# Summing the up-projection's weight blocks in device memory for the second MLP too, and running it with two plain groups instead of three

## The chip, the cores and the metric

The kernel runs on one core of one Trainium2 chip. All inputs and the output lie in device memory. The metric is the device time of one execution in microseconds (us); for the kernel before, three runs gave 1130.71, 1130.74 and 1131.74 us, so the median is 1130.74.

The engines that matter are PE (TensorE, matrix products), DVE (VectorE) and ACT (ScalarE) for elementwise work, and POOL (GpSimd) and SP (SyncE), which here issue DMAs. A DMA that SP issues copies. A DMA that POOL issues can also add what it reads to what is at the destination (`accum_op=ALU.add`); the page calls the queue of POOL's DMAs q0 and that of SP's DMAs q1.

## The reference, cut to what matters

512 tokens of width 1024 pass two layers. Layer 0 has an attention mixer, layer 1 a gated short convolution; after each comes an MLP with a causal width-3 convolution along the tokens between its up-projection and its gate:

```
def causal_dwconv(x, w):                       # x (1, 512, n), w (3, n)
    xp = pad(x, two zeros ahead of the tokens)
    return sum(xp[:, j:j + 512] * w[j] for j in range(3))

def conv_ffn(h, norm_g, w_up, conv_w, w_down): # w_up (1024, 5632), w_down (2816, 1024)
    u = causal_dwconv(rms_norm(h, norm_g) @ w_up, conv_w)
    g, val = u[..., :2816], u[..., 2816:]
    return (silu(g) * val) @ w_down

for layer in range(2):
    h = h + (attention_mixer(h) if layer == 0 else short_conv_mixer(h))
    h = h + conv_ffn(h, ffn_norm[layer], ffn_w_up[layer], ffn_conv[layer], ffn_w_down[layer])
```

Everything is float32. `ffn_w_up[layer]` holds the gate's columns in its first 2816 and the value's in its last 2816.

## The kernel before, in words

**Products in three parts.** A float32 operand is split into a high part (ACT copies it into a tile of the reduced type) and a low part (DVE subtracts). A product is then three matmuls: high by high, high by low, low by high. Weights arrive by a DMA of SP in a float32 tile `raw` (three buffers, `load`, L286); ACT makes `whi` (L292), DVE makes `wlo` (L293).

**The up-projection of an MLP** (`up_seven`, L1198) goes over 11 groups of 256 gate columns and the 256 value columns that belong to them. Some groups at the beginning are plain: four times (two column tiles, gate and value) eight steps over the width of 1024, each three matmuls of 128x128 weights by 512 tokens (`mm3`, L313 to L315), so 96 matmuls of 512 columns. The other groups go by seven products instead of eight: the tokens are cut in two halves, the width in two halves of 512, and of the group's four weight blocks (upper or lower half of the width; gate or value) and the four blocks of the activations sums are made, such that seven products of half size give the whole (`seven`, L1039, the matmul is L1045). One of the seven has 24 matmuls of 256 columns; a group has 168. `Sevens.slot(g, s)` (L1116) writes down slot s of group g; the slots are in the order p1, p7, p3 (of the group before), p6, p2, q5, q4. `PLAIN = 2, 3` says how many groups are plain in layer 0 and in layer 1.

**The sums of weight blocks** of a group are: p7 takes (lower, value) plus (upper, value); p6 takes that plus (upper, gate); q4 takes that plus (lower, gate); q5 takes (upper, gate) plus (upper, value); p1, p2 and p3 take single blocks. They are made in one of two ways:

- In layer 1 and in the short convolution, in SBUF: SP loads `X` (upper, gate) and `Y` (lower, or upper, value); a DMA of POOL adds the other value block to `Y` (`add_block`, L1072); DVE adds `X` to `Y` for p6 (L1102) and `W` to `Y` for q4 (L1155).
- In layer 0, in device memory ahead of time: `table_steps` (L85) makes the tables "7", "6" and "4" with 36 DMAs of POOL. The nine groups 2 to 10 form three chunks of three groups, a chunk has two row halves, and each of these six parts is a chain of six DMAs of 768 KB, each of which works on what the one before left: copy a block into "7", add a block, copy "7" into "6", add, copy "6" into "4", add. It is a generator; the loop over the attention's units (L946 to L948) takes two steps a time. SP then loads `Y`, `p6 sum` and `q4 sum` from the tables, L1061 and L1069.

In both ways the sum for q5 is made in SBUF: when the weights of p1 and p7 are taken from `X` and `Y`, POOL adds a block to `X` (`first_sums`, L1103, the DMA is L1072); later `weights_of(g, "q5", "X")` (L1160) makes high and low of it.

**What sets the order.** Each engine and each DMA queue works in the order in which its instructions were written down. `pin` (keep_in_program_order) holds POOL's DMAs, and SP's loads of a group that uses tables, in the order of the program. An instruction of POOL that issues a DMA waits first until the data that it needs has landed; what is behind it on POOL waits too. Elementwise work that needn't be done at a fixed place ("chores": convolution, gate, the sums of the activations' blocks in `prepare`, L1240) is taken in small pieces between matmuls, by a budget of microseconds (`work_off`; `SHARE`, and `rate` per slot).

**Around the plain groups** (L1275 to L1299). In layer 0 the results of the second plain group stay in PSUM banks (`bank(("ab", "ab", "bb", "cc")[j][half])`) and their chores come at the end of the list; the wide tiles of the last plain group lie in the place `hs_a` of the plain groups' operands (`wides_of`, L1213). In layer 1 the chores of all three plain groups are put on the list as they come. At the last plain product, `weights_of(base, "p1", "X")` and `first_sums(base)` are written down.

**The stages**, in order: attention; MLP 0 (`mlp(0)`: up-projection, then the down-projection, also by seven products, L1598); the short convolution (`conv_seven`, L1303: eight plain products, then four groups by seven products), its output projection (eight plain products), MLP 1 (`mlp(1)`), whose last results go out.

Of the kernel before, what the change touches and what calls it, by code (L numbers as in the profile page):

```python
# [25 lines left out]
P = 128  # L26
# [19 lines left out]
NSUMS, NROWS, LATE = 4.0, 3.0, 7.0  # L46
FILL1, FILL2, BEFORE = 1.5, 3.3, 2.0
UNITS = (0, 1), (2,), (3,)
PLAIN = 2, 3
CHUNKS = (2, 3), (5, 3), (8, 3)  # L50
SHARE = 0.58

# [2 lines left out]
def trunk(  # L55
# [26 lines left out]

    tables = {}

    def table_steps():  # L85

        w = ffn_w_up[0]
        for n in "764":
            for g, m in CHUNKS:
                tables[n, g] = far.tile([512, m * 256 + 16], F32, tag=f"t{n}{g}", name=f"t{n}{g}")  # L90
        def block(kh, half, g, m):
            return w[kh * 512:(kh + 1) * 512, half * DFF + g * 256:half * DFF + (g + m) * 256]
        for g, m in CHUNKS:
            for rows in (slice(0, 256), slice(256, 512)):
                for step in range(6):
                    n = "764"[step // 2]
                    to = tables[n, g][rows, 0:m * 256]
                    if step % 2:
                        src = block(*((0, 1), (0, 0), (1, 0))[step // 2], g, m)
                        pin(nc.gpsimd.dma_start(to, src[rows, :], accum_op=ALU.add))  # L100
                    else:
                        src = block(1, 1, g, m) if step == 0 else tables["76"[step // 2 - 1], g][:, 0:m * 256]
                        pin(nc.gpsimd.dma_start(to, src[rows, :]))
                    yield

    def table_of(n, group):
        g, m = next(c for c in CHUNKS if c[0] <= group < c[0] + c[1])
        return tables[n, g][:, (group - g) * 256:(group - g + 1) * 256].rearrange("(k p) c -> p k c", p=P)

    work_scope = ExitStack()  # L110
    work = work_scope.enter_context(tc.tile_pool(name="work", bufs=2))
# [345 lines left out]
    def want_ffn(layer, pairs=NF):  # L457
        for j in range(pairs):
            want(ffn_w_up[layer], 0, 8, j * P, P)
            want(ffn_w_up[layer], 0, 8, DFF + j * P, P)  # L460
# [8 lines left out]
    def want_conv_out():  # L469
        for o in range(ND):  # L470
            want(conv_w_out[0], 0, 8, o * P, P)
        want_ffn(1, 2 * PLAIN[1])

    want_ffn(0, 2 * PLAIN[0])

    def products(acc, w, order=tuple(range(ND))):
        for k in order:
# [462 lines left out]
            fillers.append(values(g + 1))  # L940
    units = [(p, u) for p in range(8) for u in range(len(UNITS))]
    waiting = {}
    sums_far = table_steps()
    next(sums_far)
    fill(PRE)
    for g in range(len(units) + 2):  # L946
# [13 lines left out]
        if 1 <= g <= len(units):  # L960
            for b, w in waiting.pop(g - 1):
                turn(units[g - 1][0], b, w)
                fill(FILL2 / len(UNITS[units[g - 1][1]]))
    fill(1e9)

    def residual_out(o, acc, nxt):
        dve.tensor_tensor(h[:, o, :], acc, h[:, o, :], op=ALU.add)
# [230 lines left out]
    def up_seven(layer, norm, mp):  # L1198

        blocks = Blocks(mp, layer)  # L1200
        w_up, base = ffn_w_up[layer], PLAIN[layer]

        def block_of(g, kh, half):
            c0 = half * DFF + 2 * g * P
            return w_up[kh * 512:(kh + 1) * 512, c0:c0 + 2 * P].rearrange("(k p) c -> p k c", p=P)

        up = Sevens(layer, mp, range(base, HF), block_of)
        up.norm, up.chores = norm, []
        if layer == 0:
            up.table = table_of  # L1210
            up.rate = lambda g, s: 1.4 if g == base else 0.5

        def wides_of(g):  # L1213
            if layer == 0 and g == base - 1:
                t = hsp.tile([P, 8, S], F32, tag="hs_a", name=f"hs_a_wide{layer}")
                return {n: t[:, 2 * i:2 * i + 2, :] for i, n in enumerate(("yg", "yv", "ug", "uv"))}
            return {n: mp.tile([P, 2, S], F32, tag=n, name=f"{n}{layer}{g}", bufs=1) for n in ("yg", "yv", "ug", "uv")}
        up.wides_of = wides_of
        wides, forms, chores = up.wides, up.forms, up.chores

        def taps_of(g, half, i):
            return lambda j: ffn_tap(layer, j, half * NF + 2 * g + i)

        def conv(g, half, i):
            src, dst = (wides[g][n[half]] for n in (("yg", "yv"), ("ug", "uv")))
# [12 lines left out]
        up.tail = tail  # L1238

        def prepare(half):  # L1240
            k0 = 2 * half
            x0, x1, s = (
                mp.tile([P, 2, S], F32, tag=t, name=f"{t}_prep{layer}{half}", bufs=b) for t, b in (("X", 2), ("px", 1), ("Y", 2)))
            for x, f in ((x0, k0), (x1, k0 + 4)):
                for i in range(2):
                    dve.scalar_tensor_tensor(x[:, i, :], h[:, f + i, :], gain_of(norm.base, f + i), norm.row, op0=ALU.mult, op1=ALU.mult)
                    yield 0.75
            s0, s1 = s[:, :, LEFT], s[:, :, RIGHT]
            a, b, c, d = x0[:, :, LEFT], x0[:, :, RIGHT], x1[:, :, LEFT], x1[:, :, RIGHT]
            for n, src, made in (("p1", a, None), ("p7", s0, (a, b, ALU.subtract)), ("p6", s0, (s0, d, ALU.add)), ("p2", c, None),  # L1250
                                 ("q5", s1, (b, d, ALU.subtract)), ("q4", d, None), ("p3", s0, (c, s0, ALU.subtract))):
                if made:
                    dve.tensor_tensor(src, made[0], made[1], op=made[2])
                    yield 0.69
                halves_to(*(t[:, k0:k0 + 2, :] for t in forms[n]), src)
                yield 0.69

        def normed(g, i, accs):
            if i == 0:
                up.open_wides(g)  # L1260
            for acc, n in zip(accs, ("yg", "yv")):
                dve.tensor_tensor(wides[g][n][:, i, :], acc, norm.row, op=ALU.mult)
                yield 0.69

        def gate_one(g, i):
            u = [wides[g][n] for n in ("ug", "uv")]
            for half in range(2):
                conv(g, half, i)
                yield 1.5
            act.activation(u[0][:, i, :], u[0][:, i, :], AF.Silu)  # L1270
            blocks.product(2 * g + i, 1, u[0][:, i:i + 1, :], u[1][:, i:i + 1, :])
            yield 0.86

        kept = []
        for j in range(2 * base):  # L1275
            accs = []
            for half in range(2):
                accs.append(bank(("ab", "ab", "bb", "cc")[j][half] if layer == 0 else "ab"[half]))
                for _ in products(accs[-1], weights()):
                    up.work_off(SHARE)  # L1280
                if j == 2 * base - 1 and half == 1:
                    up.weights_of(base, "p1", "X")
                    up.first_sums(base)
            if j == 2 * base - 2:
                up.load_pair(base)
                if not up.table:
                    up.add_block(base, "Y", 1, 1)
            kept.append(accs)
            if layer == 0:
                if j < 2:  # L1290
                    chores.extend((normed(0, j, accs), prepare(j)))
                continue
            chores.append(normed(j // 2, j % 2, accs))
            if j in (0, 2):
                chores.append(prepare(j // 2))
            for i in {1: (0, 1), 3: (2, 3), 4: (4,), 5: (5,)}.get(j, ()):
                chores.append(gate_one(i // 2, i % 2))
        if layer == 0:
            chores.extend([gate_one(0, i) for i in range(2)] + [normed(1, i, kept[2 + i]) for i in range(2)] + [gate_one(1, i) for i in range(2)])  # L1299
        slots = [(lambda g=g, s=s: up.slot(g, s)) for g in range(base, HF + 1) for s in range(7)]  # L1300
        return blocks, slots

    def conv_seven(norm, mp):  # L1303
# [109 lines left out]
        for j in range(8):  # L1413
# [9 lines left out]
            if j == 5:  # L1423
                up.load_pair(1)
                up.add_block(1, "Y", 1, 1)
            if j == 7:
                up.weights_of(1, "p1", "X")
                up.first_sums(1)
                up.weights_of(1, "p6", "Y")
        want_conv_out()  # L1430
        for s in range(28):
            up.slot(1 + s // 7, s % 7)
            if s == 27:
                fetch(1)
        for s in (0, 2, 3):
# [5 lines left out]
    def mlp(layer, norm, mp):  # L1441
# [21 lines left out]
        def block(kh, ch, k0, fresh):  # L1463
            return (ffn_w_down[layer], kh * HF + k0, ch * 512), fresh
# [37 lines left out]
                else:  # L1502
                    pin(dve.tensor_tensor(b, b, d, op=ALU.add))

        n_up = 7 * (HF - PLAIN[layer])
        for i, fn in enumerate(slots[:n_up]):
            fn()
            left = n_up - i
# [177 lines left out]
```

## Time and profile before

| | |
|---|---|
| median of three runs | 1130.74 us |
| the profiled execution, its own time | 1129.42 us |
| its span on the core | 1127.5 us |
| PE busy | 1116.9 us (99%), 7619 matmuls |
| DVE, ACT busy | 948.9 us (84%), 674.8 us (60%) |
| POOL busy (work, and issuing as far as counted) | 150.3 us (13%) |
| granted PE clock | 0.9 or more of full speed in all 40 slices |
| DMAs of POOL (q0) | 71.74 MB, 33.8% of the 16 engines' span |
| DMAs of SP (q1) | 116.37 MB, 33.2% |

Rows of the timeline have the start (us from the span's beginning), the length (us), engine and line, the operation with the tile it writes and what it reads, a count where neighbours were merged, and in brackets how long the engine had been idle before and what ended this. Matmuls overlap: a row of 512 columns is 0.39 us long, but the next starts 0.23 us later, and with 256 columns 0.28 us and 0.12 us. The starts, not the lengths, give the pace. Rows of a list of DMA issues have the count, the size of each, and the median us from issue to landing. Lines are those of the kernel before.

### The profile page before, as it was taken

How to read it: one execution, taken by the hardware profiler on the slowest of the kernel's cores; microseconds unless marked ns; L12 is line 12 of the kernel's file. 1: busy time of each engine (PE TensorE's matmuls, PEld its weight loads, DVE VectorE, ACT ScalarE, POOL GpSimd, SP SyncE). 2: the span in 40 equal slices, each digit the busy share in tenths (PEclk: the TensorE clock that was granted, in tenths of full speed). 3: DMA queues.
4: the chain of work that ended last, by engine and by line, in shares of the span. 5: the costliest groups of instructions: out<-in, count | busy, mean ns of one | idle time of the engine just before them, and what ended most of it. 6: DMA issues, size and time to landing. Idle time of an engine off the chain costs nothing.

```text
span 1127.5 us, 19238 instructions
## 1 busy us (share of the span) xinstructions
PE 1116.9 (99%) x7619; PEld 1007.1 (89%) x7619; DVE 948.9 (84%) x1447; ACT 674.8 (60%) x1006; POOL 150.3 (13%) x174
## 2 busy tenths in 40 slices
PE   8999999999999999999999999999999999999998
PEld 7888787878899999999999899988889999998886
DVE  6787888887899787888989889865898899998886
ACT  7556676655466666676557355543445666677553
POOL 4011111110001110014400001000012111014300
PEclk9999999999999999999999999999999999999999
DMA  6678767674368777799953455543275876789961
GB/s 194 173 179 204 187 170 198 154 204 123 88 179 206 201 198 195 202 287 204 224 164 91 127 138 132 113 122 96 83 195 114 177 182 151 180 234 211 227 157 56
DMA packets 171689, 189.40 MB, mean 168 GB/s; under 512 B 7148, under 2 KB 140828, under 8 KB 171600
## 3 DMA queue, kind: packets, MB, share of 16 engines
q0 software_dynamic: 39728, 71.74, 33.8%
q1 hardware_dynamic: 131712, 116.37, 33.2%
q8 instruction: 59, 0.97, 0.3%
q14 instruction: 30, 0.25, 0.1%
q10 hardware_dynamic: 160, 0.07, 0.0%
HBM read 183.18 MB, written 30.41 MB: 189 GB/s over the span
## 4 chain that ended last, share of the span: by engine, by line
PE 90%; DVE 5%; ACT 2%; DMA 2%; issue 1%; DVEq 0%; ACTq 0%; POOLq 0%
PE psb L1045 23%; PE psb L1598 11%; PE psa L1045 9%; PE psa L1598 8%; PE psb L313 6%; PE psb L314 6%; PE psb L315 6%; PE psa L315 3%; PE psa L313 3%; PE psa L314 3%; DMA Xc<-in_conv_w_in 2%; PE psa L784 2%; PE psb L688 2%; PE psb L570 1%; PE psb L571 1%
## 5 line engine op out<-in xcount | busy, mean ns | idle before, releaser
L292 ACT ACTIVATE whi<-raw 128x1024 fp32r<-128x1024 f32 (+2 forms) x93 | 95.8, 1032 | 93.9 <-PE psb L314 29.0
L293 DVE TENSOR_TENSOR wlo<-raw,whi 128x1024 fp32r<-128x1024 f32 (+2 forms) x93 | 110.4, 1188 | 25.3 <-ACT whi L292 24.4
L1045 PE MATMUL psb<-p_lo,whi_p 128*128 128x256 f32 x408 | 114.8, 281 | 0.0
L1045 PE MATMUL psb<-p_hi,wlo_p 128*128 128x256 f32 x408 | 114.8, 281 | 0.0
L1045 PE MATMUL psb<-p_hi,whi_p 128*128 128x256 f32 x408 | 114.5, 281 | 0.0
L313 PE MATMUL psb<-hs_a,whi 128*128 128x512 f32 x240 | 98.5, 410 | 0.0
L315 PE MATMUL psb<-hs_a,wlo 128*128 128x512 f32 x240 | 95.0, 397 | 0.0
L1045 PEld LDWEIGHTS psb<-p_hi,whi_p 128*128 128x128 f32 x408 | 77.3, 189 | 0.0
L1045 PEld LDWEIGHTS psb<-p_lo,whi_p 128*128 128x128 f32 x408 | 76.8, 188 | 0.0
L1045 PE MATMUL psa<-p_hi,wlo_p 128*128 128x256 f32 x272 | 76.8, 282 | 0.0
L1045 PEld LDWEIGHTS psb<-p_hi,wlo_p 128*128 128x128 f32 x408 | 76.7, 188 | 0.0
L1045 PE MATMUL psa<-p_lo,whi_p 128*128 128x256 f32 x272 | 76.5, 281 | 0.0
L1045 PE MATMUL psb<-q_lo,whi_q 128*128 128x256 f32 x272 | 76.5, 281 | 0.0
L1045 PE MATMUL psb<-q_hi,wlo_q 128*128 128x256 f32 x272 | 76.5, 281 | 0.0
L1045 PE MATMUL psa<-p_hi,whi_p 128*128 128x256 f32 x272 | 76.3, 281 | 0.0
L1045 PE MATMUL psb<-q_hi,whi_q 128*128 128x256 f32 x272 | 76.3, 281 | 0.0
L1598 PE MATMUL psb<-act,whi 128*128 128x256 f32 x352 | 63.1, 282 | 0.1
L423 DVE SCALAR_TENSOR_TENSOR uv<-yv,taps,uv 128x511 f32<-128x511 f32 (+1 forms) x84 | 59.8, 746 | 0.2
L423 DVE SCALAR_TENSOR_TENSOR ug<-yg,taps,ug 128x511 f32<-128x511 f32 (+1 forms) x84 | 59.0, 747 | 0.3 <-ACT ug L420 0.3
L1598 PE MATMUL psb<-whi,act 128*128 128x512 f32 x176 | 56.6, 398 | 0.0
L1598 PEld LDWEIGHTS psb<-act,whi 128*128 128x128 f32 x352 | 54.2, 189 | 0.5 <-DVE act L995 0.3
L315 PEld LDWEIGHTS psb<-hs_a,wlo 128*128 128x128 f32 x240 | 45.1, 188 | 10.5 <-DVE wlo L293 0.2
(480 smaller groups left out, 3635.7 us busy)
## 6 DMA issues: line engine op xcount, KB each, us to landing
t<-in_ffn_w_up POOLq DMA_DIRECT2D x24, 768.0 KB, 7.4
raw<-in_attn_w_in SPq DMA_DIRECT2D x24, 512.0 KB, 5.0
raw<-in_ffn_w_up SPq DMA_DIRECT2D x20, 512.0 KB, 3.9
t<-t POOLq DMA_DIRECT2D x12, 768.0 KB, 4.9
X<-in_ffn_w_up SPq DMA_DIRECT2D x17, 512.0 KB, 4.9
W<-in_ffn_w_up SPq DMA_DIRECT2D x17, 512.0 KB, 4.6
X<-in_ffn_w_up POOLq DMA_DIRECT2D x17, 512.0 KB, 7.7
Z<-in_ffn_w_up SPq DMA_DIRECT2D x17, 512.0 KB, 4.5
```

The source lines that it names most:

```text
L292: return (act.activation(hi[:, at_], raw[:, at_], AF.Copy), dve.tensor_tensor(lo[:, at_], raw[:, at_], f32(hi[:, at_]), op=ALU.subtract))
L293: dve.tensor_tensor(lo[:, at_], raw[:, at_], f32(hi[:, at_]), op=ALU.subtract))
L313: made = [pe.matmul(acc, w[0], rhs[0], start=first, stop=False), pe.matmul(acc, w[0], rhs[1], start=False, stop=False), pe.matmul(acc, w[1 ...
L314: pe.matmul(acc, w[0], rhs[1], start=False, stop=False),
L315: pe.matmul(acc, w[1], rhs[0], start=False, stop=last)]
L423: dve.scalar_tensor_tensor(dst[:, d:], src[:, 0:S - d], tap(j), dst[:, d:], op0=ALU.mult, op1=ALU.add)
L570: pe.matmul(acc, lhs[0], w[0], start=first, stop=False)
L571: pe.matmul(acc, lhs[0], w[1], start=False, stop=False)
L688: pe.matmul(ss[e][:, c:c + wide], ql[rows, b * P:n], kl[rows, 0:wide], start=first and b == bs[0], stop=last and b == bs[-1])
L784: pe.matmul(out_, w, t[:, first:first + step * (NB - k - 1) + 1:step, :], start=k == 0 and i == 0, stop=k == NB - 1 and i == 1)
L1045: pe.matmul(to, w[a][:, k, c], x[b][:, k, :], start=fresh and i + k + t == 0, stop=i == 1 and k == 3 and t == 2, skip_group_check=not fresh)
L1598: pe.matmul(to, l, r, start=begin and o + t == 0, stop=end and t == 2 and o == (0 if layer else 1), skip_group_check=not fresh)
```

## The change

- `PLAIN` is 2 for both layers: the third group of layer 1's up-projection, 96 matmuls of 512 columns, becomes a group by seven products.
- `table_steps(layer)` makes a second set of nine tables from `ffn_w_up[1]`, in 36 further DMAs of POOL of 768 KB each. They are written down at three places, `FAR = 9, 9, 18` at a time: behind the attention's loop; in `conv_seven`, in plain product j = 5, behind the `add_block` of the first group's `Y` (L1425); and in `conv_seven` behind slot 20, which is slot 6 of group 3, the place where the last `first_sums` of the convolution stands.
- Layer 1's up-projection takes its sums from these tables as layer 0 does: SP loads `Y`, `p6 sum` and `q4 sum`; the DMAs of POOL that added to `Y` and the two additions of DVE a group go away. The addition to `X` for q5 stays on POOL.
- Layer 1 takes over layer 0's order around the plain groups: the banks, the place of the wide tiles, the order of the chores and the `rate`; SP's loads there are pinned.

```diff
-PLAIN = 2, 3
+PLAIN = 2
+FAR = 9, 9, 18
...
-    def table_steps():
+    def table_steps(layer):
 
-        w = ffn_w_up[0]
+        w = ffn_w_up[layer]
         for n in "764":
             for g, m in CHUNKS:
-                tables[n, g] = far.tile([512, m * 256 + 16], F32, tag=f"t{n}{g}", name=f"t{n}{g}")
+                tables[layer, n, g] = far.tile([512, m * 256 + 16], F32, tag=f"t{layer}{n}{g}", name=f"t{layer}{n}{g}")
...
-        want_ffn(1, 2 * PLAIN[1])
+        want_ffn(1, 2 * PLAIN)
...
     fill(1e9)
+
+    run(sums_far)
+    sums_far = table_steps(1)
+
+    def sum_far(n):
+        for _ in range(n):
+            next(sums_far, None)
+
+    sum_far(FAR[0])
...
-        if layer == 0:
-            up.table = table_of
-            up.rate = lambda g, s: 1.4 if g == base else 0.5
+        up.table = lambda n, g: table_of(layer, n, g)
+        up.rate = lambda g, s: 1.4 if g == base else 0.5
 
         def wides_of(g):
-            if layer == 0 and g == base - 1:
+            if g == base - 1:
...
-                accs.append(bank(("ab", "ab", "bb", "cc")[j][half] if layer == 0 else "ab"[half]))
+                accs.append(bank(("ab", "ab", "bb", "cc")[j][half]))
...
             if j == 2 * base - 2:
                 up.load_pair(base)
-                if not up.table:
-                    up.add_block(base, "Y", 1, 1)
             kept.append(accs)
-            if layer == 0:
-                if j < 2:
-                    chores.extend((normed(0, j, accs), prepare(j)))
-                continue
-            chores.append(normed(j // 2, j % 2, accs))
-            if j in (0, 2):
-                chores.append(prepare(j // 2))
-            for i in {1: (0, 1), 3: (2, 3), 4: (4,), 5: (5,)}.get(j, ()):
-                chores.append(gate_one(i // 2, i % 2))
-        if layer == 0:
-            chores.extend([gate_one(0, i) for i in range(2)] + [normed(1, i, kept[2 + i]) for i in range(2)] + [gate_one(1, i) for i in range(2)])
+            if j < 2:
+                chores.extend((normed(0, j, accs), prepare(j)))
+        chores.extend([gate_one(0, i) for i in range(2)] + [normed(1, i, kept[2 + i]) for i in range(2)] + [gate_one(1, i) for i in range(2)])
...
             if j == 5:
                 up.load_pair(1)
                 up.add_block(1, "Y", 1, 1)
+                sum_far(FAR[1])
...
         for s in range(28):
             up.slot(1 + s // 7, s % 7)
+            if s == 20:
+                sum_far(FAR[2])
```

More of the change, by code (lines that the diff above doesn't have):

```diff
@@ L96, in table_steps @@
                     n = "764"[step // 2]
-                    to = tables[n, g][rows, 0:m * 256]
+                    to = tables[layer, n, g][rows, 0:m * 256]
                     if step % 2:
@@ L101, in table_steps, with table_of @@
                     else:
-                        src = block(1, 1, g, m) if step == 0 else tables["76"[step // 2 - 1], g][:, 0:m * 256]
+                        src = block(1, 1, g, m) if step == 0 else tables[layer, "76"[step // 2 - 1], g][:, 0:m * 256]
                         pin(nc.gpsimd.dma_start(to, src[rows, :]))
                     yield
-    def table_of(n, group):
+    def table_of(layer, n, group):
         g, m = next(c for c in CHUNKS if c[0] <= group < c[0] + c[1])
-        return tables[n, g][:, (group - g) * 256:(group - g + 1) * 256].rearrange("(k p) c -> p k c", p=P)
+        return tables[layer, n, g][:, (group - g) * 256:(group - g + 1) * 256].rearrange("(k p) c -> p k c", p=P)
     work_scope = ExitStack()
@@ L471, in want_conv_out @@
             want(conv_w_out[0], 0, 8, o * P, P)
-        want_ffn(1, 2 * PLAIN[1])
-    want_ffn(0, 2 * PLAIN[0])
+        want_ffn(1, 2 * PLAIN)
+    want_ffn(0, 2 * PLAIN)
     def products(acc, w, order=tuple(range(ND))):
@@ L942, in trunk @@
     waiting = {}
-    sums_far = table_steps()
+    sums_far = table_steps(0)
     next(sums_far)
@@ L1200, in up_seven @@
         blocks = Blocks(mp, layer)
-        w_up, base = ffn_w_up[layer], PLAIN[layer]
+        w_up, base = ffn_w_up[layer], PLAIN
         def block_of(g, kh, half):
@@ L1503, in sums @@
                     pin(dve.tensor_tensor(b, b, d, op=ALU.add))
-        n_up = 7 * (HF - PLAIN[layer])
+        n_up = 7 * (HF - PLAIN)
         for i, fn in enumerate(slots[:n_up]):
```

## The prediction

> **What bounds the kernel now.** First the page: span, busy time, and the chain of work that ended last.
>
> ```profile
> span 1127.5 us, 19238 instructions
> ...
> PE 1116.9 (99%) x7619; PEld 1007.1 (89%) x7619; DVE 948.9 (84%) x1447; ACT 674.8 (60%) x1006; POOL 150.3 (13%) x174
> ...
> PE 90%; DVE 5%; ACT 2%; DMA 2%; issue 1%; DVEq 0%; ACTq 0%; POOLq 0%
> ```
>
> PE is busy 99% of the span. So only two things can move the time: fewer or shorter matmuls, or a wait of PE that isn't there now. Work taken from DVE, 84% busy, gives nothing by itself.
>
> Second, PE's timeline at the borders of the two up-projections: the first plain matmul, the first by seven products, and the first of the down-projection, of layer 0 and then of layer 1.
>
> ```profile
> 277.80 0.39 PE L313 MATMUL psb<-hs_a,whi 128*128 128x512 f32 x1
> 323.79 0.28 PE L1045 MATMUL psa<-p_hi,whi_p 128*128 128x256 f32 x1
> 499.95 0.28 PE L1598 MATMUL psa<-act,whi 128*128 128x256 f32 x1
> ...
> 784.42 0.40 PE L313 MATMUL psa<-hs_a,whi 128*128 128x512 f32 x1
> 852.79 0.28 PE L1045 MATMUL psa<-p_hi,whi_p 128*128 128x256 f32 x1
> 1009.12 0.39 PE L1598 MATMUL psa<-whi,act 128*128 128x512 f32 x1
> ```
>
> Layer 0, with two plain groups and tables, takes 499.95 - 277.80 = 222.15 us. Layer 1, with three and none, takes 1009.12 - 784.42 = 224.70 us. Layer 1 after the change is layer 0's code on other weights, so this pair prices the main edit.
>
> Third, POOL's timeline: first and last of the 36 table DMAs of now, and the DMAs of POOL that border its idle stretches.
>
> ```profile
> 40.30 0.58 POOL L103 DMA_DIRECT2D t<-in_ffn_w_up  x1
> ...
> 257.60 0.89 POOL L100 DMA_DIRECT2D t<-in_ffn_w_up  x1 [6.24 <-DMA t<-t]
> 323.37 1.35 POOL L1072 DMA_DIRECT2D X<-in_ffn_w_up  x1 [64.88 <-DVE wlo_p L995]
> ...
> 596.81 1.28 POOL L1072 DMA_DIRECT2D Yc<-in_conv_w_in  x1 [34.77 <-DVE wlo L293]
> 661.71 1.28 POOL L1072 DMA_DIRECT2D Xc<-in_conv_w_in  x1 [63.62 <-DVE Yc L1102]
> ...
> 719.48 1.28 POOL L1072 DMA_DIRECT2D Xc<-in_conv_w_in  x1 [16.40 <-DVE Yc L1102]
> 822.98 1.20 POOL L1037 DMA_DIRECT2D head<-head  x1 [102.22 <-issue]
> ```
>
> The brackets are the three idle stretches: 64.88, 63.62 and 102.22 us. A table DMA occupies POOL for 0.6 or 0.9 us of work, but the next of its chain waits on POOL until it has landed (the bracket of the second row), and so does whatever stands behind it.
>
> **The change part by part.** *The plain group and the borrowed order.* 96 matmuls of 512 columns go, 168 of 256 columns come. By the two stages this gives 222.15 - 224.70 = -2.55 us, with the norm's small matmuls, the tail and the other order of chores in both. No PE stall enters by layer 0's order: its 45.99 us for two plain groups are 2/3 of layer 1's 68.37 plus 0.4.
>
> *SBUF sums.* Eight `Y` additions by POOL and sixteen additions of DVE leave layer 1. They lie beside PE, which doesn't wait for them: nothing. SP gets two more loads a group and another source for `Y`, as in layer 0: nothing, since layer 0's stage is already in the sum.
>
> *The 36 table DMAs.* PE doesn't see them unless a later DMA of POOL stands behind one. How long a chain of six takes is read where now's run, second chain and the steps next to it:
>
> ```profile
> 46.94 0.99 POOL L100 DMA_DIRECT2D t<-in_ffn_w_up  x1 [6.05 <-DMA t<-in_ffn_w_up]
> ...
> 72.51 0.89 POOL L100 DMA_DIRECT2D t<-in_ffn_w_up  x1 [4.62 <-DMA t<-t]
> 73.08 0.88 POOL L103 DMA_DIRECT2D t<-in_ffn_w_up  x1
> 81.62 0.94 POOL L100 DMA_DIRECT2D t<-in_ffn_w_up  x1 [7.66 <-DMA t<-in_ffn_w_up]
> 88.83 0.58 POOL L103 DMA_DIRECT2D t<-t  x1 [6.26 <-DMA t<-in_ffn_w_up]
> 93.93 0.88 POOL L100 DMA_DIRECT2D t<-in_ffn_w_up  x1 [4.53 <-DMA t<-t]
> ```
>
> The first copy of a chain is issued 0.57 us behind the last addition of the chain before, beside which it takes 8.54 us (73.08 to 81.62; alone 6.64, 40.30 to 46.94). An addition takes 7.21, a copy of a table 5.10. A chain little disturbed: 0.57 + 8.54 + 7.21 + 5.10 + 7.21 + 5.10 = 33.7 us. The six chains of now take 257.60 + 0.57 - 40.30 = 217.9 us, 36.3 each; undisturbed they would be 6 x 33.7 - 1.9 (the first copy is alone) = 200.3. The 17.6 us between go to loads of SP that share the DMA engines. SP's timeline counts them:
>
> ```profile
> 45.84 123.07 SPq L286 DMA_DIRECT2D raw<-in_attn_w_in  x14
> 174.49 64.92 SPq L286 DMA_DIRECT2D raw<-in_attn_w_out  x8
> 249.92 42.59 SPq L286 DMA_DIRECT2D raw<-in_ffn_w_up  x8
> 300.77 0.37 SPq L1060 DMA_DIRECT2D X<-in_ffn_w_up  x1
> ...
> 326.70 0.37 SPq L1069 DMA_DIRECT2D Z<-in_ffn_w_up  x1
> ...
> 613.61 14.30 SPq L286 DMA_DIRECT2D raw<-in_conv_w_in  x5
> ...
> 644.86 0.50 SPq L1060 DMA_DIRECT2D Xc<-in_conv_w_in  x1
> ...
> 720.71 33.91 SPq L286 DMA_DIRECT2D raw<-in_conv_w_out  x8
> 758.78 63.38 SPq L286 DMA_DIRECT2D raw<-in_ffn_w_up  x12
> ```
>
> 14 + 8 + 2 = 24 loads lie between 40 and 258 us, so a load costs the chain 17.6 / 24 = 0.73 us.
>
> *First stretch*: nine steps behind 257.60. Up to the issue of the ninth 8.54 + 7.21 + 5.10 + 7.21 + 5.10 + 0.57 + 8.54 + 7.21 = 49.5 us, and 11 loads (six of the eight `raw`, and five of those that begin at 300.77) at 0.73, 8 us: POOL is free at 317. Its next DMA, `X` of layer 0's first group, is ready at 323.37. Nothing, with 6 us to spare; if that cover were gone, each us would be one of PE (below).
>
> *Second stretch*: nine steps behind 598.1, the chain's fourth first: 7.21 + 5.10 + 0.57 + 8.54 + 7.21 + 5.10 + 7.21 + 5.10 = 46.0 us, and 9 loads (613.61 to 644.86), 6.6: free at 652, needed at 661.71. Nothing.
>
> *Third stretch*: eighteen steps, three whole chains, behind 719.48 + 1.28 = 720.76. The next DMA on POOL is no longer `head` at 822.98, it is `X` of layer 1's first group by seven products, which comes a plain group earlier than now. By layer 0's order it is ready 323.37 - 277.80 = 45.57 us behind the first plain matmul, at 784.42 + 45.57 = 829.99. Loads of SP until then: 8 of `conv_w_out`, 8 of `ffn_w_up` (of the 12), and the eight from `X` to `Z` that in layer 0 lie 23 to 49 us behind the first plain matmul: 24, as many in about 115 us as the attention has in 218. Three chains: 3 x 33.7 + 24 x 0.73 = 118.6 us. The last addition is issued 0.57 earlier, and takes 0.9: POOL is free at 720.76 + 118.6 - 0.57 + 0.9 = 839.7, 9.7 us late.
>
> What hangs on `X` is read in layer 0, where this addition lands in
>
> ```profile
> X<-in_ffn_w_up POOLq DMA_DIRECT2D x1, 512.0 KB, 7.5
> ```
>
> and high and low of it are made for q5:
>
> ```profile
> 331.12 1.05 ACT L993 ACTIVATE whi_q<-X 128x1024 fp32r<-128x1024 f32 x1
> ...
> 332.39 1.22 DVE L995 TENSOR_TENSOR wlo_q<-X,whi_q 128x1024 fp32r<-128x1024 f32 x1
> ...
> 335.25 0.28 PE L1045 MATMUL psb<-q_hi,whi_q 128*128 128x256 f32 x1
> ```
>
> The low part is there at 333.61; the third matmul of q5, which needs it, is due at 335.5. So `X` may land 1.9 us behind the 331.12 at which ACT takes it, which is 784.42 + 55.2 = 839.6 in layer 1. It lands at 839.7 + 7.5 + 1.9 (issued beside an addition, as 8.54 against 6.64) = 849.1. PE waits 9.5 us; ACT and DVE stand behind the same wait, so nothing is caught up.
>
> The Trainium skill, "DMA: Bandwidth & Descriptors", section "Anatomy of one DMA — SWDGE (gpsimd) path", fits a DMA of POOL as 2.0 us and its bytes at 436 GB/s, which is 3.8 us for 768 KB, an estimate. By it eighteen steps in a row take 68 us, POOL is free ahead of 790, and the sum is -2.55. This trace has 5.10 for the table's copy and 7.21 for the addition, so the rows stand.
>
> *Sum*: -2.55 + 9.5 = +6.9 us. The profiled execution has 1129.42, so 1136.4 on its own scale; the median of the runs is 1.3 higher. I put 1136.5.
>
> **The bounds of the unknown price**, a load's cost to a step. Below: nothing, then POOL is free at 822, and no wait is left. Above: the whole time a load keeps the engines. A window over 720 to 784 us gives it:
>
> ```profile
> q1 hardware_dynamic: 13412, 6.77, 36.4%
> ...
> raw<-in_conv_w_out SPq DMA_DIRECT2D x8, 512.0 KB, 4.4
> raw<-in_ffn_w_up SPq DMA_DIRECT2D x5, 512.0 KB, 3.9
> ```
>
> 36.4% of 64 us for 13 loads is 1.8 us each. I take 0.73, the mean of 24 loads beside the same DMAs. No gain beyond -2.55 is possible: PE has no idle time to lose.
>
> **The rivals.**
>
> *No wait (the other side).* The third stretch goes at the attention's own 36.3 us a chain: POOL is free at 720.76 + 108.9 + 0.3 = 830, `X` lands at 839.4, inside the slack, and the time is 1130.74 - 2.55 = 1128.2. For it: 36.3 is measured beside real loads, and chains of now went as fast as 32.2 (40.30 to 72.51). Against it: nearly twice as many loads per us. It decides at POOL free at 830. This is also how the skill's fit would have it; the trace doesn't bear that out.
>
> *A small wait*, 0.3 to 4.8 us, from a price of 0.35 to 0.53 a load: 1128.5 to 1133.
>
> *The whole 1.8 us a load*: 24 x 1.07 = 26 us more, a wait of 35 and about 1163; the first stretch would then end behind 323.37 as well. Against it: 0.73 in the attention. The Trainium skill, same page, section "Issuing engines are not separate DMA queues", says that DMAs of all issuing engines run on the same 16 engines and interleave. The trace agrees that loads and steps delay each other (36.3 against 33.7 a chain).
>
> *PE loses nothing by the extra loads themselves*, I hold: SP's `raw` at 758.78 is for a product that begins at 784.42, 25 us later.
>
> **How the numbers follow.** About 0.2%, 2.26 us, is what a measurement tells from no change here. A wait over 4.8 us, POOL free behind 835: 0.55, likeliest 1136.5, by itself 1133 to 1146 (up to 1.1 us a load). The whole price, or a wait in an earlier stretch: 0.07. A small wait: 0.14. No wait: 0.24, at -2.55 just over the bound. So faster 0.24, same 0.14, slower 0.62. The range takes in the side without a wait: 1127.8 to 1146.5.
>
> **What would show it.** Right: on POOL an `X` of L1072 near 840 whose idle time ends with a table DMA; on ACT `whi_q<-X` waiting for `X` near 849; PE's first q5 some 9 us late, once; L1045 beginning at about 830.4; the up-projection otherwise at layer 0's 222 us. Wrong: the eighteen steps end ahead of 830; or the first two stretches run over, with PE waiting at the first q5 of layer 0 or of the convolution; or the -2.55 doesn't come, since layer 1 in layer 0's order leaves PE waiting for something else.

## The result and the profile after

The changed kernel takes 1142.07 us (median of 6 runs, 1141.21 to 1146.25) against 1131.12 for the kernel before beside it. The ratio is 1.0104, with a 95% interval of 1.0086 to 1.0122. It is slower by about 11 us. The direction was forecast, the size was not: +5.8 us stood in the forecast.

In the rows of the changed kernel the lines have moved: the matmuls by seven products are L1055 (L1045 before), `add_block` is L1082 (L1072), the plain matmuls L314 to L316, the down-projection L1600. The page of its profiled execution (1142.31 us), with span, busy time, granted clock and chain:

```profile
span 1140.5 us, 19427 instructions
...
PE 1117.3 (98%) x7691; PEld 1010.5 (89%) x7691; DVE 932.6 (82%) x1430; ACT 679.0 (60%) x1013; POOL 167.9 (15%) x203
...
PEclk9999999999999999999999999999989999999999
...
PE 71%; DMA 12%; DVE 9%; issue 4%; ACT 3%; POOL 0%; DVEq 0%; SPq 0%; ACTq 0%; POOLq 0%
```

PE is as busy as before in us, but the span is 13 us longer: time in which PE waits. The chain now has 12% DMA where it had 2%, and one slice has a lower clock. PE's timeline at the same borders as in the prediction:

```profile
278.08 0.39 PE L314 MATMUL psb<-hs_a,whi 128*128 128x512 f32 x1
324.07 0.28 PE L1055 MATMUL psa<-p_hi,whi_p 128*128 128x256 f32 x1
501.55 0.28 PE L1600 MATMUL psa<-act,whi 128*128 128x256 f32 x1
...
788.29 0.40 PE L314 MATMUL psa<-hs_a,whi 128*128 128x512 f32 x1
834.34 0.28 PE L1055 MATMUL psa<-p_hi,whi_p 128*128 128x256 f32 x1
1022.51 0.39 PE L1600 MATMUL psa<-whi,act 128*128 128x512 f32 x1
```

From such starts, the lengths of the stages in us (here and for the experiments below, each from one profiled execution):

| kernel | to MLP 0 | up 0 | down 0 | conv, plain and sevens | conv out | up 1 | down 1 |
|---|---|---|---|---|---|---|---|
| before | 277.8 | 222.2 | 112.8 | 127.0 | 44.7 | 224.7 | 114.4 |
| changed | 278.1 | 223.5 | 113.7 | 128.4 | 44.7 | 234.2 | 113.9 |
| 9, 9, 13 and five later | 278.2 | 222.8 | 113.1 | 128.9 | 44.7 | 222.9 | 113.9 |
| first X by SP and DVE | 278.2 | 222.5 | 112.9 | 129.3 | 44.7 | 223.4 | 114.1 |
| sums in SBUF, no tables | 277.6 | 222.8 | 113.1 | 127.5 | 44.7 | 224.2 | 114.0 |
| tables, three plain groups | 277.8 | 222.8 | 113.5 | 128.6 | 44.7 | 225.3 | 114.4 |
| tables for three groups | 278.2 | 222.2 | 112.8 | 127.1 | 44.7 | 223.0 | 113.9 |

Of the 12.9 us between the two profiled executions 9.5 are in MLP 1's up-projection, and 3.6 in up 0, down 0 and the convolution. PE's waits, the longest group first, say what it is (total, times, longest):

```profile
PE psb L1055 <- ACT Xs L1107: 10.5, 2, 9.4
```

Nothing like this stood in the kernel before. The name is that of the last ACT instruction ahead of it; ACT itself waited for `X`. POOL's timeline around the two first `X` additions:

```profile
321.84 0.58 POOL L104 DMA_DIRECT2D t<-t  x1 [7.62 <-DMA t<-in_ffn_w_up]
323.66 1.35 POOL L1082 DMA_DIRECT2D X<-in_ffn_w_up  x1 [1.24 <-DVE wlo_p L1005]
...
724.46 1.15 POOL L104 DMA_DIRECT2D t<-in_ffn_w_up  x1
...
833.01 0.59 POOL L104 DMA_DIRECT2D t<-t  x1 [6.39 <-DMA t<-in_ffn_w_up]
839.32 0.87 POOL L101 DMA_DIRECT2D t<-in_ffn_w_up  x1 [5.72 <-DMA t<-t]
839.88 1.67 POOL L1082 DMA_DIRECT2D X<-in_ffn_w_up  x1
```

The eighteenth table DMA of the third stretch is issued at 839.32, and `X` at once behind it, without idle time: it had been ready before. The last instruction that reads `X` ahead of the addition ends at 830.99, as DVE's timeline shows:

```profile
829.77 1.22 DVE L1005 TENSOR_TENSOR wlo_p<-X,whi_p 128x1024 fp32r<-128x1024 f32 x1
```

The addition's landing and its use, from the list of issues, ACT's timeline and PE's:

```profile
X<-in_ffn_w_up POOLq DMA_DIRECT2D x1, 512.0 KB, 11.6
```

```profile
851.54 1.06 ACT L1003 ACTIVATE whi_q<-X 128x1024 fp32r<-128x1024 f32 x1 [9.68 <-DMA X<-in_ffn_w_up]
```

```profile
843.00 0.28 PE L1055 MATMUL psa<-p_lo,whi_p 128*128 128x256 f32 x1
843.12 0.60 PE L1525 MATMUL psc<-ident,h 128*128 128x128 f32 x4
853.14 0.58 PE L1055 MATMUL psb<-q_hi,whi_q 128*128 128x256 f32 x1 [9.42 <-ACT Xs L1107]
853.52 0.41 PE L1055 MATMUL psb<-q_lo,whi_q 128*128 128x256 f32 x1
853.73 0.41 PE L1055 MATMUL psa<-p_hi,wlo_p 128*128 128x256 f32 x1
```

The section on the kernel before has each engine work in the order written down. For PE that isn't so here, and the order isn't layer 0's either. In layer 0 all 24 matmuls of p2 (`psa<-p`) stand ahead of q5 (`psb<-q`). Here two of them are followed by four transposes of the residual (L1525), which the kernel's text has in the down-projection, and by two matmuls of q5. The other 22 of p2, 2.6 us of work whose operands don't depend on `X`, stand behind the wait.

And PE's busy time, the other engines' and the granted clock in three windows (columns: length, PE, PEld, DVE, ACT, POOL busy, the clock, share of the DMA engines, GB/s): during the wait, the 4.6 us behind it, and then:

```profile
845.00:853.00 8.00, 0.00 (x0) 0.00 (x0) 0.37 (x1) 1.46 (x3) 0.00 (x0) 0.64 1.03 193
853.00:857.60 4.60, 4.46 (x21) 4.46 (x22) 4.40 (x7) 1.55 (x3) 0.00 (x0) 0.51 0.22 55
857.60:865.00 7.40, 7.40 (x64) 7.40 (x64) 5.32 (x8) 4.52 (x6) 1.31 (x1) 1.00 0.78 211
```

Behind the wait the clock is 0.51, and 20 matmuls start 0.21 us apart instead of 0.12: 20 x 0.094 = 1.9 us more.

### The profile page after: what moved, and what is told of

It is laid out like the page before. It is cut to its first block, busy times and chain, and to the rows that moved or that the text cites. A ratio compares the mean times of both kernels' runs of the same rounds, so it can differ in the third digit from the quotient of the medians.

```text
span 1140.5 us, 19427 instructions
## 1 busy us (share of the span) xinstructions
PE 1117.3 (98%) x7691; PEld 1010.5 (89%) x7691; DVE 932.6 (82%) x1430; ACT 679.0 (60%) x1013; POOL 167.9 (15%) x203
## 4 chain that ended last, share of the span: by engine, by line
PE 71%; DMA 12%; DVE 9%; issue 4%; ACT 3%; POOL 0%; DVEq 0%; SPq 0%; ACTq 0%; POOLq 0%
PE psb L1055 22%; PE psb L1600 10%; PE psa L1055 8%; PE psa L1600 8%; DMA t<-in_ffn_w_up 5%; PE psb L314 3%; PE psb L315 3%; PE psb L316 3%; DMA t<-t 2%; DMA Xc<-in_conv_w_in 2%; DMA X<-in_ffn_w_up 2%; PE psb L689 1%; PE psa L785 1%; PE psa L314 1%; PE psa L316 1%
## 5 line engine op out<-in xcount | busy, mean ns | idle before, releaser
L1055 PE MATMUL psb<-p_lo,whi_p 128*128 128x256 f32 x432 | 121.6, 281 | 0.0
L1055 PE MATMUL psb<-p_hi,wlo_p 128*128 128x256 f32 x432 | 121.6, 281 | 0.0
L1055 PE MATMUL psb<-p_hi,whi_p 128*128 128x256 f32 x432 | 121.2, 281 | 0.0
L314 PE MATMUL psb<-hs_a,whi 128*128 128x512 f32 x224 | 92.2, 412 | 0.0
L1055 PE MATMUL psb<-q_hi,whi_q 128*128 128x256 f32 x288 | 81.2, 282 | 10.5 <-ACT Xs L1107 10.5
L316 PE MATMUL psb<-hs_a,wlo 128*128 128x512 f32 x224 | 88.7, 397 | 0.0
L1055 PEld LDWEIGHTS psb<-p_hi,whi_p 128*128 128x128 f32 x432 | 81.9, 190 | 0.0
L1055 PE MATMUL psa<-p_hi,wlo_p 128*128 128x256 f32 x288 | 81.9, 284 | 0.0
L1055 PE MATMUL psa<-p_lo,whi_p 128*128 128x256 f32 x288 | 81.8, 284 | 0.0
L1055 PE MATMUL psa<-p_hi,whi_p 128*128 128x256 f32 x288 | 81.6, 283 | 0.0
L1055 PEld LDWEIGHTS psb<-p_lo,whi_p 128*128 128x128 f32 x432 | 81.3, 188 | 0.0
L1055 PEld LDWEIGHTS psb<-p_hi,wlo_p 128*128 128x128 f32 x432 | 81.2, 188 | 0.0
L1055 PE MATMUL psb<-q_lo,whi_q 128*128 128x256 f32 x288 | 81.2, 282 | 0.0
L1055 PE MATMUL psb<-q_hi,wlo_q 128*128 128x256 f32 x288 | 81.0, 281 | 0.0
L101 POOL DMA_DIRECT2D t<-in_ffn_w_up x36 | 33.0, 916 | 222.0 <-DMA t<-t 121.9
L1055 PEld LDWEIGHTS psb<-q_hi,whi_q 128*128 128x128 f32 x288 | 54.7, 190 | 10.9 <-ACT Xs L1107 10.9
L1600 PE MATMUL psb<-act,whi 128*128 128x256 f32 x352 | 63.1, 282 | 0.1
L1600 PE MATMUL psb<-whi,act 128*128 128x512 f32 x176 | 56.3, 397 | 0.0
```

What stands on the lines that cost most here:

```text
L314: made = [pe.matmul(acc, w[0], rhs[0], start=first, stop=False), pe.matmul(acc, w[0], rhs[1], start=False, stop=False), pe.matmul(acc, w[1 ...
L316: pe.matmul(acc, w[1], rhs[0], start=False, stop=last)]
L1055: pe.matmul(to, w[a][:, k, c], x[b][:, k, :], start=fresh and i + k + t == 0, stop=i == 1 and k == 3 and t == 2, skip_group_check=not fresh)
L1600: pe.matmul(to, l, r, start=begin and o + t == 0, stop=end and t == 2 and o == (0 if layer else 1), skip_group_check=not fresh)
```

## The experiments

Three theories were set against each other. **Queue**: `X` of MLP 1's first group stands on POOL behind the table DMAs, and this wait, with the slow PE behind it, is most of the loss. **Traffic**: the tables' bytes fill the DMA engines they share with everything else, and the order on POOL doesn't matter. **Order**: it says that layer 1 in layer 0's order leaves PE waiting by itself.

### Five table DMAs out of the third stretch

```diff
-FAR = 9, 9, 18
+FAR = 9, 9, 13
+LATER = {1: 1, 8: 1, 15: 1, 22: 1, 29: 1}
...
             fn()
+            if layer:
+                sum_far(LATER.get(i, 0))
```

(in `mlp`, behind the up-projection's slot i)

> Edit: 13 of the third stretch's 18 table DMAs stay there, the other five are taken one at a time between the slots of MLP 1, behind the addition to X of a group; nothing else of the change is touched. Theory 'queue' (X of MLP 1's first group stands on POOL behind the table DMAs; its 9.4 us of waiting and some 1.9 us of slow PE behind it are most of the loss): POOL is free at about 805 to 815 us, no wait of PE at that q5, and 11.3 us less than the changed kernel: about 1130.8, within 0.1% of the kernel before; the wait of about 1 us at layer 0's first q5 stays. Rival 'traffic' (the tables' bytes on the shared DMA engines delay whatever is loaded, in whatever order POOL stands): the bytes are the same and are only moved to the busiest stage, so at most 3 us are won, 1139 or more.

Measured: 1129.73 us, 0.9987 of the kernel before (0.9978 to 0.9996). POOL's timeline: thirteenth table DMA, then `X`; and ACT's use of it.

```profile
799.29 0.89 POOL L105 DMA_DIRECT2D t<-in_ffn_w_up  x1
830.60 1.33 POOL L1083 DMA_DIRECT2D X<-in_ffn_w_up  x1 [30.42 <-DVE wlo_p L1006]
```

```profile
841.08 1.04 ACT L1004 ACTIVATE whi_q<-X 128x1024 fp32r<-128x1024 f32 x1
```

`X` is issued when its own data lets it, 30 us of idle POOL ahead of it, and ACT doesn't wait. The same 36 DMAs and bytes, five of them moved into MLP 1, and 12 us are gone. Traffic, which allowed 3, is out as the cause of the loss. The wait at layer 0's first q5, which was expected to stay, isn't in this execution.

### The first X not on POOL

```diff
-            self.add_block(g, "X", 0, 1)
+            if self.name == 1 and g == PLAIN:
+                self.load_one(g, "V", self.block_of(g, 0, 1))
+                dve.tensor_tensor(self.st[g]["X"], self.st[g]["X"], self.st[g]["V"], op=ALU.add)
+            else:
+                self.add_block(g, "X", 0, 1)
```

> Edit: only for MLP 1's first group by seven products the block that is added to X is loaded by SP and added by DVE (one more addition of 1.2 us), not by a DMA of POOL; all eighteen table DMAs stay in the third stretch. Theory 'queue': the table DMAs end near 840 us as before, but PE's wait at that q5 is gone, about 11 us less than the changed kernel, 1130 to 1132; DVE's extra addition may cost up to 1 us. Rival 'traffic': SP's load runs beside the same table DMAs and is late as well; a wait of 4 us or more stays, 1135 or more.

Measured: 1130.17 us, 0.9990 (0.9982 to 0.9999). The end of the table DMAs on POOL, and ACT:

```profile
839.34 0.59 POOL L104 DMA_DIRECT2D t<-t  x1 [7.85 <-DMA t<-in_ffn_w_up]
845.91 0.87 POOL L101 DMA_DIRECT2D t<-in_ffn_w_up  x1 [5.98 <-DMA t<-t]
```

```profile
840.97 1.05 ACT L1003 ACTIVATE whi_q<-X 128x1024 fp32r<-128x1024 f32 x1
```

The table DMAs end at 846, later even than in the changed kernel, and `X` is there at 841, beside them. So it is the place on POOL's queue. One addition of DVE replaces a wait of 9 us. PE's order around q5 changed too, all of p2 stands ahead of it here, but the high part of `X` is there at 842.0, ahead of the 842.8 at which the changed kernel's order would have come to q5.

### Two plain groups without tables

```diff
-FAR = 9, 9, 18
+FAR = 0, 0, 0
...
-        up.table = lambda n, g: table_of(layer, n, g)
+        if layer == 0:
+            up.table = lambda n, g: table_of(layer, n, g)
...
                 up.load_pair(base)
+                if not up.table:
+                    up.add_block(base, "Y", 1, 1)
```

> Edit: two plain groups and layer 0's order in MLP 1, but no second set of tables at all: its sums are made in SBUF as before (two additions of DVE and one more DMA of POOL a group). Theory 'queue' (the group's exchange is worth its 2.55 us, and only the table DMAs spoil it): about 1128.5 where DVE has room for its two additions, and some us more if it has none in the first group by seven products, where layer 0 has DVE at 19.8 of 20 us. Rival 'order' (layer 1 in layer 0's order leaves PE waiting by itself): 1131 or more, with a wait at the first products by seven.

Measured: 1129.94 us, 0.9992 (0.9984 to 1.0001): 1.2 us less by the medians, not told apart from no change by the interval. One wait of PE is new, at the first group by seven products:

```profile
PE psa L1055 <- DVE wlo_p L1005: 1.0, 1, 1.0
```

DVE is busy for all of the 10 us up to it, as feared, and the two more additions are the likely cause of this 1 us. Up 1 falls only to 224.2, but the order theory, in its strong form, is out: without tables the exchange costs nothing. The 1128.5 of the queue theory did not come either.

### Fewer table DMAs in the first and the third stretch

`FAR = 7, 9, 14`, and six DMAs one at a time between the slots of MLP 1.

> Edit: 7, 9 and 14 table DMAs in the three stretches, and six one at a time between the slots of MLP 1. Theory 'queue': neither the first q5 of layer 0 nor that of layer 1 waits, so the exchange of the group shows: 1131.1 - 2.55 = 1128.6, up to 1129.6 with the small waits that stand in the changed kernel elsewhere. Rival 'traffic': above 1133, as the bytes are the same. Rival 'order': no waits at X, and still 1131.

Measured: 1130.28 us, 0.9994 (0.9985 to 1.0002). No wait at either first q5, and up 0 at the 222.1 of the kernel before. But no faster than with 9, 9 and 13: taking two DMAs from the first stretch won nothing that shows, and the 1128.6 did not come. The convolution's two stages still took 128.0.

### The tables with three plain groups

The kernel before, `table_steps(layer)`, `FAR = 9, 9, 18` and the tables used in layer 1; plain groups and order as before.

> Edit: the kernel before with the second set of tables alone: 9, 9 and 18 table DMAs at the same places, MLP 1's sums taken from them, but three plain groups and its own order. X of its first group by seven products is ready at about 853 us, behind the end of the table DMAs near 840. Theory 'queue': no wait at that q5; what is left is what the table DMAs cost in the first two stretches, 1 to 2 us by the stage times of the runs so far (the convolution's stages took 128 to 129 us with tables and 127.0 to 127.5 without), so 1132 to 1133.5. Rival 'traffic': the same bytes, so most of the 11 us, 1138 or more.

Measured: 1132.98 us, 1.0013 (1.0004 to 1.0022): 1.6 us more, inside what was expected. The second set of tables alone costs this where its wait finds cover. In the profiled execution most of the difference sits in the first stages of the table above.

### Seventeen

`FAR = 9, 9, 17`, and the eighteenth behind `X` of MLP 1's first group.

> Edit: 17 instead of 18 table DMAs in the third stretch; the eighteenth is taken behind X of MLP 1's first group. In the changed kernel the seventeenth is issued at 833.01 us, and X is ready at about 833.9. Theory 'queue', to the step: X is issued at once (not behind the landing of the seventeenth, 6.4 us) and has nothing but a table's copy beside it (landing 7.5 to 9.4 instead of 11.6), so the wait of 9.4 us falls to between 0 and 1 us, the slow PE behind it goes too, and one DMA moved is worth 10 to 11 us: 1130 to 1132. Rival 'traffic': one of 36 DMAs fewer ahead of X takes an eighteenth of it, 0.6 us: 1141 or more.

Measured: 1137.81 us, 1.0049 (1.0030 to 1.0068), but with runs from 1131.47 to 1141.11. Neither expectation is right. In the profiled execution (1140.38 us) POOL's timeline has:

```profile
838.75 0.59 POOL L105 DMA_DIRECT2D t<-t  x1 [7.24 <-DMA t<-in_ffn_w_up]
839.32 1.37 POOL L1083 DMA_DIRECT2D X<-in_ffn_w_up  x1
844.72 0.93 POOL L102 DMA_DIRECT2D t<-in_ffn_w_up  x1 [4.03 <-DMA t<-t]
```

The chain of copies and additions went slower in this execution, the seventeenth came at 838.75 and not at 833, and `X` was as late as before: a wait of 9.5 us. The expectation had taken the 833.01 of one execution for fixed. In the six profiled executions with eighteen in this stretch the seventeenth was issued between 833.0 and 840.1, which is enough to decide whether PE waits. That would also spread the runs as they are spread, by 9.6 us against 1.6 in the version with tables for three groups below; no profile of a faster run shows it.

### Tables for the first three groups only

```diff
-FAR = 9, 9, 18
+FAR = 0, 0, 12
...
         up.table = lambda n, g: table_of(layer, n, g)
+        up.by_table = lambda g: layer == 0 or g < 5
```

(and in `Sevens` each question whether there is a table is put to the group; the later six groups of layer 1 make their sums in SBUF)

> Edit: two plain groups; tables in layer 1 for the first three groups by seven products only (12 DMAs, all in the third stretch), the later six groups make their sums in SBUF as before. Nothing stands in the first two stretches. Theory 'queue' with a cost of the second stretch of about 1 us: the table DMAs end near 810, no wait at any q5, the convolution's stages at the kernel before's, MLP 1's up-projection at 222.2 to 223: 1128.5 to 1129.2, the fastest of all. If the second stretch costs nothing: as the version with 9, 9, 13 and five later, 1129.7. If DVE has no room for the sums of the later groups: 1130 or more, with waits of PE for low parts.

Measured: 1128.48 us (1127.70 to 1129.26), 0.9971 (0.9960 to 0.9981): 2.9 us less than the kernel before, and the lowest median here; the interval still touches that of 9, 9 and 13. POOL, twelfth table DMA and `X`:

```profile
797.03 0.87 POOL L102 DMA_DIRECT2D t<-in_ffn_w_up  x1 [4.31 <-DMA t<-t]
828.20 1.33 POOL L1083 DMA_DIRECT2D X<-in_ffn_w_up  x1 [30.30 <-DVE wlo_p L1006]
```

With nothing in the second stretch the convolution is back at 127.1. What the nine DMAs do there is read in ACT's waits and in the landings of SP's loads over some 25 and 40 us from its beginning, first of the changed kernel:

```profile
ACT whi L293 <- DMA raw<-in_conv_w_in: 3.9, 2, 3.2
```

```profile
raw<-in_conv_w_in SPq DMA_DIRECT2D x5, 512.0 KB, 7.8
```

and of this version, where ACT never waits for such a load:

```profile
raw<-in_conv_w_in SPq DMA_DIRECT2D x5, 512.0 KB, 4.3
```

A weight that lands at 7.8 us instead of 4.3 holds ACT, then DVE's `wlo`, and behind that on DVE the short instructions of the norm, for which PE waits. DVE's timeline and PE's waits in the changed kernel:

```profile
627.05 1.23 DVE L294 TENSOR_TENSOR wlo<-raw,whi 128x1024 fp32r<-128x1024 f32 x1 [0.77 <-ACT whi L293]
```

```profile
PE psc L374 <- DVE ncol_n L412: 0.7, 1, 0.7
```

This wait of PE, 0.5 to 0.7 us, is in all eight profiled executions with nine table DMAs in each of the first two stretches, and in none of the three without any in the second. With 7, 9 and 14 it is missing, and the convolution took 128.0 all the same. In this narrow sense the traffic theory is right: the convolution pays 1 to 2 us. How the rest of it arises beside this wait was not followed up.

### A busy wait

The changed kernel, with matmuls on constants ahead of q5 of MLP 1's first group, the result unused:

```diff
+                if s == 5 and self.name == 1 and g == PLAIN:
+                    t = bank("c")
+                    for _ in range(44):
+                        pe.matmul(t, ident16, begin, start=True, stop=True)
                 self.product(g, form, n, fresh)
```

> Edit: the changed kernel with 44 matmuls on constants (512 columns, some 9.5 us, their result unused) written down between p2 and q5 of MLP 1's first group by seven products, so that PE is busy while it waits for X. The wait itself stays. Theory 'idle makes PE slow': in the changed kernel's trace 20 matmuls behind the wait stand 0.213 us apart instead of 0.119; here they stand at 0.119 from the first, and the time is about 1.9 us less than the changed kernel's. Rival 'the slow pace comes from what PE reads or from the DMA engines': it stays slow for 4 us, and the time is that of the changed kernel.

> The changed kernel itself, on the same chip as the one with a busy wait, for their comparison: 1.0104 of the kernel before, within 0.002.

Measured: 1.0112 (1.0090 to 1.0133) with the busy wait, and 1.0105 (1.0091 to 1.0119) for the changed kernel again, on the same chip. By the time nothing is decided. In the profiled execution of the changed kernel again PE waited 11.4 us at q5, not 9.4, and 14 matmuls behind the wait were slow, not 20. In that with the busy wait `X` was later still, ACT waited 14.85 us for it, and PE stood idle for 2.9 us after the 44. The windows from there (as above):

```profile
851.00:857.20 6.20, 3.34 (x15) 1.37 (x14) 0.42 (x1) 1.51 (x3) 0.00 (x0) 1.00 0.88 139
857.20:859.20 2.00, 1.65 (x11) 1.44 (x12) 1.79 (x2) 2.00 (x5) 0.00 (x0) 1.00 0.00 0
859.20:862.80 3.60, 3.60 (x20) 3.60 (x19) 3.60 (x7) 1.61 (x3) 0.00 (x0) 0.53 0.57 143
862.80:880.00 17.20, 17.20 (x147) 17.20 (x147) 14.87 (x20) 11.99 (x16) 1.30 (x1) 1.00 0.72 184
```

PE begins q5 at full pace and becomes slow 2 us later, for 3.6 us. So with 72 such matmuls, which outlast the wait:

> Edit: as the version with a busy wait, with 72 matmuls (15.5 us), more than the wait is long, so that PE has no idle time at all ahead of q5. One look at the trace, since the matmuls now outlast the wait and the time says nothing. Theory 'idle makes PE slow': no matmul of q5 stands 0.213 us behind the one before, and the granted clock stays at 1.00 over the 20 us behind the wait. Rival 'the slow pace comes from what PE reads or from the DMA engines': the same 0.213 us for some 3 to 4 us.

Measured, one execution (1145.15 us): no slow matmul at all.

```profile
840.00:860.00 20.00, 20.00 (x112) 11.61 (x111) 8.08 (x11) 5.68 (x8) 3.45 (x3) 1.00 0.73 147
860.00:880.00 20.00, 20.00 (x170) 19.97 (x170) 14.55 (x19) 11.71 (x15) 1.30 (x1) 1.00 0.60 155
```

So the slow pace comes with PE's idle time. What PE reads is the same, and the DMA engines are no rival: in the 4.6 us from the start of q5 they are busier here than behind the wait of the changed kernel (a share of 1.05 against 0.22), and PE is not slow. It is one execution.

## Why the prediction was right in its direction and wrong in its size

**The exchange, -2.55.** Confirmed, a little smaller. Up 1 falls by 1.7 to 1.8 us with 9, 9 and 13 and with tables for three groups. Four transposes of the residual moved from the down-projection into the up-projection, so both stages count together: -2.2 us in both.

**The first stretch, "nothing, with 6 us to spare".** POOL was free at 322.4 and not at 317, still ahead of the `X` at 323.66. But a table copy was in flight beside it, `X` landed in 10.8 us and not in 7.5, and PE waited 1 us in this execution; in seven others with the same nine there, up 0 took 222.1 to 222.8. The prediction's step from POOL being free in time to "Nothing, with 6 us to spare" left out what is still under way in front of the next DMA.

**The second stretch, "nothing".** POOL was free at 653 as worked out (652). The step that failed is another: "PE doesn't see them unless a later DMA of POOL stands behind one", and with it "PE loses nothing by the extra loads themselves". I priced what a load costs a table DMA, 0.73 us, and never what a table DMA costs a load; the rows of before (36.3 against 33.7 a chain) showed only the one side. I looked only at `raw` of MLP 1, loaded 25 us ahead; in the convolution a load is used sooner. In every version with table DMAs in the second stretch the convolution's two stages took 128.0 to 129.3 us; in those without, 127.0 to 127.5.

**The third stretch.** Right in its mechanism: `X` of L1082 near 840, ACT waiting for `X`, one late q5. POOL was to be free at 839.7, and `X` was issued at 839.88; the wait was to be 9.5 and was 9.4. That the size agrees is luck, since two differences cancel.

The stretch began 3.7 us later than assumed, since the stages ahead were longer, and its chains took (839.32 + 0.57 - 724.46) / 3 = 38.5 us, not 39.5. So `X` was issued only 0.2 behind the 839.7 at which POOL was to be free. `X` landed in 11.6 us and not in 9.4, which makes 2.2 more. The moment by which ACT had to take `X` came 2.5 later, at 842.1 and not at 839.6: 3.9 for the longer stages, less 1.4 because PE came to q5 sooner than by layer 0's order, with 22 matmuls of p2 behind it. "Layer 1 after the change is layer 0's code" holds for the text, not for PE's order. `X` itself was ready at 831.0, where layer 0's distance gave 833.9. And the changed kernel's second profiled execution waited 11.4 us.

**The term that was missing.** Behind the wait PE runs at half pace for 4 us, 1.9 us in all; in the second profiled execution of the changed kernel it is 3 us and 1.4. Nothing in the sum stood for it, and no reason was given. The profile of before can't show it, as the longest wait among PE's waits there is 1.3 us. The Trainium skill, "TensorE: Matmul & The Clock Gate", section "Part 1: The HAM clock gate (the "warmup" mystery)", says that the clock falls to half after an idle window of about 3.4 us and comes back after as long a busy one. The trace agrees: 0.51 over 4.6 us behind 9.4 us of idle time, and none behind the wait that was filled. In the execution with 44 matmuls in the wait it doesn't: there 2.9 us of idle time were followed by the half clock too (0.53).

**Together.** -2.2 + 9.4 + 1.9 = 9.1 us in MLP 1 (9.0 by the starts). Between the two profiled executions up 0, down 0 and the convolution add 3.6 and attention 0.3, which makes their 12.9. The version without any table in layer 1 has 1.4 of the 3.6 as well, though its first stages are those of the kernel before, so about that much is how one execution differs from the next, and by the medians the whole is 11.0. How much of the 3.6 the table DMAs cost in an average run stays open; the tables with three plain groups cost 1.6 in all, and 3.6 less 1.4 is 2.2.

So the steps that failed are two terms put at nothing: the half pace behind the wait, 1.4 to 1.9 us, and the table DMAs' cost to the loads and to the additions beside them in the first two stretches, some 1.6 to 2.2 us. A third is a slip of scale: the sum had +6.9, and 1136.5 is that sum on the profiled execution's scale; on the median's it is 1137.7.

**The rivals.** No wait: wrong, though one DMA fewer brings some runs near the time of the kernel before (1131.5). A figure for it was read too low: the 32.2 us of a fast chain end at the issue of its last addition; the next chain starts at 32.8, and the first copy had nothing beside it. A small wait: wrong in the two profiled executions of the changed kernel (9.4 and 11.4 us). The whole 1.8 us a load: far off.

## What to carry to other kernels

DMAs that wait for each other don't fill a queue's idle time, they occupy the queue: ahead of each chain stands the question what the next instruction behind it is, when it will be ready after the change, and how many us are left. Where the sum comes to a few us, put fewer there, or take that one instruction off the queue; twelve DMAs, for the first three groups, did what thirty-six had not. A wait of PE of 9 to 11 us is priced with the half pace behind it, here 1.4 to 1.9 us. And it is worth looking in the trace at what stands behind the waiting instruction on its engine: here 2.6 us of ready work did.

## What the runs showed of the hardware that was not expected

An addition of 512 KB by POOL that lands in 7.5 us takes 11.6 when it is issued right behind an addition of 768 KB, and 10.8 behind a copy issued 1.8 us earlier. PE's slow pace needn't begin with the first matmul behind a wait: after 2.9 us of idle time it began 2 us after the restart and lasted 3.6 us. And the time of a chain of waiting DMAs isn't steady: the seventeenth of the third stretch was issued at 833.0 us in one execution and at 838.75 in another, although that one had started 1.4 us earlier (723.07 against 724.46).
